# Three narrow matmuls become a wide and a narrow one in the recurrent mixer's input projection, and three steps of attention move

## The chip, the cores and the metric

The kernel runs on one core of one Trainium2 chip. The metric is device time in microseconds (us). The five engines named in the traces are PE (TensorE, matrix products; PEld is its weight load), DVE (VectorE), ACT (ScalarE), POOL (GpSimd) and SP (SyncE, which only issues transfers here). Each takes its instructions in order; semaphores tie the engines together.

## The reference

A trunk of two layers over 256 tokens and 2048 features, in float32. Layer 0 is attention with 16 query heads and 4 key heads of 128 features; layer 1 is a recurrent block; each is followed by a gated feed-forward part. Cut to what the change touches:

```python
h = rms_norm(x, norm_mix[i])
# layer 0
q = apply_axial_rope(rms_norm(q, q_gain), cos, sin) * (HEAD_DIM ** -0.5)   # per head
sc = jnp.einsum('bqkgd,bskd->bkgqs', q_blk, k)
p = jax.nn.softmax(sc, axis=-1);  o = jnp.einsum('bkgqs,bskd->bqkgd', p, v)
# layer 1
xb, yb = jnp.split(h @ w_in, 2, axis=-1)           # (256, 2048) @ (2048, 4096)
yb = jax.nn.gelu(yb, approximate=True)
xb = depthwise_conv_centred(xb, conv_w, conv_b)
out = (rg_lru_forward(xb) + rg_lru_backward(xb)) * yb;  mix = out @ w_out
```

## The kernel before

**Precision.** Every product is made of three: a float32 operand is split into a rounded part hi and a remainder lo, and x·w is taken as xh·wh + xl·wh + xh·wl. Weights come from memory as tiles `raw` of 128x1024 (eight 128x128 blocks; the text calls such a tile a half, since two make the 2048 rows of one projection); ACT makes `hi` (line 135), DVE makes `lo` (line 136). `raw`, `hi` and `lo` each have a ring of five buffers here. Activations lie as `xg`, a tile of 128x512 for each of 16 row blocks k, with the rounded 256 tokens in its left half and the remainders in its right half.

**Two ways to take the three products.** Attention's projections use `blocks` (lines 264 to 274): for a pair of row blocks, hi of the first against all 512 columns (line 272), lo of the first and lo of the second against the left 256 columns (line 270), hi of the second against 512. The left half of the PSUM bank then holds xh·wh, the right half xl·wh + xh·wl, and `evac` (lines 350 to 354) adds the halves: ACT copies the right half to a tile in SBUF, DVE adds the left half to it. The recurrent mixer's projection uses `project_sums` (lines 287 to 296) with `three` (lines 282 to 285): three matmuls of 256 columns for every row block, all summed in the left half of the bank, so that what follows reads the sum from PSUM. The right half is scratch for what follows.

**The recurrent mixer.** 32 column tiles of `w_in` are projected: 16 for the x branch, 16 for the gate branch y. A loop over nine rounds takes two x tiles of the next block and two y tiles of this block in each. `conv_branch` (lines 813 to 826) multiplies the projection by the row `nr.row` (1/rms of the tokens, line 818), and runs the four taps of the convolution with the bank's right half as accumulator (lines 820 to 823); `xs` is the split result. `gelu_branch` (lines 829 to 834) multiplies by the same row. Each block has four gate products (128 output columns by two, `three` again, from `xs` and the gate weights `ghi`, `glo` that POOL splits), and then sigmoids, decays and scans on ACT, DVE and POOL.

**The order.** PE's order is written by the program. A step counter goes up once for each row block in a projection; `later(n, fn)` puts a function on a list, due n steps on, and at each step at most one due entry runs, the earliest entered first. `USUAL` (line 51) holds such distances for the query heads 0 to 13: the sums of squares 17 steps after the head's projection, the scores 22 (heads 0 to 5 have 32 to 24 instead, `EARLY`), the turn of the probabilities 17 after the scores, the product with the values 8 after the turn, and the split of the query. Heads 14 and 15 have `LATE`. The other engines' order is set by a scheduler that works from estimated times.

**A query head** (`attend`, lines 623 to 684): `sums` transposes y on PE (line 639) and squares it on ACT (641); `scores` makes the scores on PE, then on DVE and ACT the head's factor f = 1/rms (648, and `rsqrt`, lines 474 to 483), the row maximum (651) times f (652), the exponentials (657, by way of 493), the reciprocal of their sums (659), the scaled probabilities `pr` (661); `turn` transposes these on PE (667) and splits them as `pT` (669, 670); `values` multiplies them by the values (675).

## Time and profile before

| | us |
|---|---|
| median of 3 runs | 1970.33 (1969.58 to 1970.8) |
| the profiled execution | 1970.78 |
| its span, first to last instruction | 1968.9 |
| query heads, about 57 to 182 us of the span | 125.0, PE busy 121.18 |
| recurrent projections and gates, 961.4 to 1191.3 us | 229.9, PE busy 229.9 |
| DVE busy in the latter | 195.53 |
| ACT busy in the latter | 191.3 |

The span begins at the first instruction on the core, and views give positions in us from there. A row of a group gives line, engine, operation, result<-operands, shapes, count, then busy time, mean duration in ns and the idle time just before. Matmuls overlap on PE: their rows give 283 or 389 ns each, but what a stream costs is the distance from start to start, so this is taken from the timeline. The granted clock is 0.999 over the run.

### The profile page before, as it was taken

Reading aid. Unit: us, or ns where it says so; the run is one execution under the profiler, and the core shown is the slowest. Engines: PE = TensorE matmul, PEld = TensorE weight load, DVE = VectorE, ACT = ScalarE, POOL = GpSimd, SP = SyncE. Lnnn points to the kernel's source line nnn. Section 1 sums busy time; section 2 is a strip of 40 time slices with the busy share of each in tenths; the row PEclk is TensorE's granted clock in tenths of the full one; section 3 lists DMA queues with packets and bytes.
Section 4 is the critical chain, followed back from the end, with each engine's and each line's share of the span. In section 5 each row is a group of like instructions: output and inputs, shape, how many; then the busy total and the mean of one; then the engine's idle time right before and its main releaser. Section 6 shows DMA issues by size and latency. Waiting matters only on the chain.

```text
span 1968.9 us, 28150 instructions
## 1 busy us (share of the span) xinstructions
PE 1957.1 (99%) x9842; PEld 1668.3 (85%) x9842; DVE 1705.4 (87%) x2254; ACT 1388.3 (71%) x2167; POOL 321.7 (16%) x395
## 2 busy tenths in 40 slices
PE   9999999999999999999999999999999999999999
PEld 8888888888888888888999998888888888888887
DVE  7877688899999999998788886897999999999993
ACT  7677586676677766777688887867667676676662
POOL 0443160000000000000456450420000000000000
PEclk9999999999999999999999999999999999999999
DMA  8544655577667776676566555656667776777763
GB/s 308 172 129 129 201 173 193 193 239 221 215 210 227 234 215 219 209 234 216 194 194 192 182 167 175 200 193 214 195 219 217 225 231 209 222 224 225 220 229 117
DMA packets 118079, 402.86 MB, mean 205 GB/s; under 512 B 13232, under 2 KB 13488, under 8 KB 117808
## 3 DMA queue, kind: packets, MB, share of 16 engines
q1 hardware_dynamic: 108432, 384.00, 59.1%
q0 software_dynamic: 9216, 16.78, 4.7%
q8 instruction: 77, 1.26, 0.3%
q14 instruction: 66, 0.54, 0.1%
q10 hardware_dynamic: 288, 0.28, 0.0%
HBM read 382.13 MB, written 2.10 MB: 195 GB/s over the span
## 4 chain that ended last, share of the span: by engine, by line
PE 91%; DVE 4%; POOL 2%; ACT 1%; issue 1%; DMA 1%; ACTq 0%; POOLq 0%; DVEq 0%
PE acc L303 16%; PE acc L304 16%; PE acc L306 16%; PE pm L306 10%; PE pm L304 10%; PE pm L303 10%; PE acc L283 3%; PE acc L284 3%; PE acc L285 3%; DVE lo L136 2%; POOL hb L569 1%; PE pm L284 1%; PE pm L285 1%; PE pm L283 1%; DMA raw<-in_w_qv_dram 0%
## 5 line engine op out<-in xcount | busy, mean ns | idle before, releaser
L136 DVE TENSOR_TENSOR lo<-raw,hi 128x1024 fp32r<-128x1024 f32 (+1 forms) x517 | 631.2, 1251 | 81.0 <-ACT hi L135 80.2
L135 ACT CAST hi<-raw 128x1024 fp32r<-128x1024 f32 (+1 forms) x517 | 527.9, 1046 | 219.3 <-DMA raw<-in_w_down_dram 101.6
L303 PE MATMUL acc<-hi,xg 128*128 128x512 f32 x844 | 328.3, 389 | 0.0
L304 PE MATMUL acc<-hi,xg 128*128 128x512 f32 x844 | 328.3, 389 | 0.0
L306 PE MATMUL acc<-lo,xg 128*128 128x512 f32 x844 | 328.3, 389 | 0.0
L153 ACT CAST hi<-ws 128x1024 fp32r<-128x1024 f32 x188 | 197.9, 1053 | 162.4 <-DVE ws L159 146.0
L156 DVE TENSOR_TENSOR lo<-ws,hi 128x1024 fp32r<-128x1024 f32 x188 | 230.5, 1227 | 35.7 <-ACT hi L153 32.4
L797 POOL DMA_DIRECT2D x<-form x64 | 55.2, 862 | 1069.9 <-ACT form L796 1069.9
L303 PE MATMUL pm<-hi,act 128*128 128x512 f32 x512 | 199.2, 389 | 0.0
L304 PE MATMUL pm<-hi,act 128*128 128x512 f32 x512 | 199.2, 389 | 0.0
L306 PE MATMUL pm<-lo,act 128*128 128x512 f32 x512 | 199.2, 389 | 0.0
L303 PEld LDWEIGHTS acc<-hi,xg 128*128 128x128 f32 x844 | 158.4, 188 | 32.9
L304 PEld LDWEIGHTS acc<-hi,xg 128*128 128x128 f32 x844 | 158.4, 188 | 32.9
L306 PEld LDWEIGHTS acc<-lo,xg 128*128 128x128 f32 x844 | 158.4, 188 | 32.9
L303 PE MATMUL acc<-hi,act 128*128 128x512 f32 x448 | 174.6, 390 | 0.0
L393 ACT COPY two<-one 32x256 f32<-32x256 f32 x420 | 169.6, 404 | 7.0 <-DVE one L385 0.8
L306 PE MATMUL acc<-lo,act 128*128 128x512 f32 x448 | 174.4, 389 | 0.0
L304 PE MATMUL acc<-hi,act 128*128 128x512 f32 x448 | 174.4, 389 | 0.0
L283 PE MATMUL acc<-xg,hi 128*128 128x256 f32 x512 | 144.8, 283 | 0.0
L284 PE MATMUL acc<-xg,hi 128*128 128x256 f32 x512 | 144.6, 282 | 0.0
L285 PE MATMUL acc<-xg,lo 128*128 128x256 f32 x512 | 144.5, 282 | 0.0
L156 DVE TENSOR_TENSOR lo<-raw,hi 128x1024 fp32r<-128x1024 f32 x94 | 114.1, 1214 | 23.0 <-ACT hi L153 23.0
(218 smaller groups left out, 3993.4 us busy)
## 6 DMA issues: line engine op xcount, KB each, us to landing
raw<-in_w_gate_dram SPq DMA_DIRECT2D x176, 512.0 KB, 4.7
raw<-in_w_up_dram SPq DMA_DIRECT2D x176, 512.0 KB, 3.9
raw<-in_w_down_dram SPq DMA_DIRECT2D x176, 512.0 KB, 4.1
raw<-in_w_in_dram SPq DMA_DIRECT2D x64, 512.0 KB, 4.4
raw<-in_w_qv_dram SPq DMA_DIRECT2D x40, 512.0 KB, 3.9
raw<-in_w_o_dram SPq DMA_DIRECT2D x32, 512.0 KB, 3.5
x<-form POOLq DMA_DIRECT2D x64, 256.0 KB, 4.8
raw<-in_w_out_dram SPq DMA_DIRECT2D x32, 512.0 KB, 4.2
```

The costliest lines, as they stand in the source:

```text
L135: behind("cast", act.copy(hi[:, sl], raw[:, sl]))
L136: behind("rest", dve.tensor_tensor(lo[:, sl], raw[:, sl], hi[:, sl].bitcast(F32), ALU.subtract))
L153: behind("cast", act.copy(hi, src))
L156: return lambda: behind("rest", dve.tensor_tensor(lo, src, hi[:].bitcast(F32), ALU.subtract))
L283: pe.matmul(o, hi, x[:, :S], start=start, stop=False)
L284: pe.matmul(o, hi, x[:, S:], start=False, stop=False)
L285: pe.matmul(o, lo, x[:, :S], start=False, stop=stop)
L303: pe.matmul(o, xh, wh, start=start, stop=False)
L304: pe.matmul(o, xl, wh, start=False, stop=False)
L306: pe.matmul(o, xh, wl, start=False, stop=stop)
L393: m = (eng.copy if eng is act else eng.tensor_copy)(to[:, :, :, i, :], of[:, :, :, j, :])
L797: pool.dma_start(out=x_tm[:, a, i[1] * WIDE : (i[1] + 1) * WIDE], in_=t, accum_op=ALU.add)
```

## The change

The input projection of the recurrent mixer goes by `blocks` as attention's does (`project`, and `project_both` for the first two tiles, which go side by side through the halves of the weights): for every pair of row blocks four matmuls, two of 512 columns and two of 256, where there were six of 256. Both halves of the bank now hold a part of the result. So each of the 32 tiles gets an `evac`: a copy of the right half by ACT and an addition by DVE into a new tile `ev` (four buffers), and the multiplication by `nr.row` reads `ev` from SBUF. The right half then serves as scratch as before.

In attention the factor f is made in `sums` and kept until `scores` takes it; and `USUAL` sets the turn 18 steps after the scores (17 before) and the values 9 after the turn (8 before). f's instructions stay the same in number.

```diff
-USUAL = (17, 22, 17, 8, 9)
+USUAL = (17, 22, 18, 9, 9)
...
-    def project_sums(xs, n):
-        banks = [new_acc() for _ in range(n)]
+    def project_both(xs):
+        banks = [new_acc() for _ in range(2)]
         for k0 in range(0, KT, HALF):
             wts = [narrow() for _ in banks]
-            for i in range(0, HALF, HALF // n):
+            for i in range(0, HALF, HALF // 2):
                 for bank, wt in zip(banks, wts):
-                    for k in range(k0 + i, k0 + i + HALF // n):
-                        three(bank[:, :S], *wt[k - k0], xs[k], k == 0, k == KT - 1)
-                        step()
-        return [(bank[:, :S], bank[:, S:]) for bank in banks]
+                    blocks(bank, wt[i : i + HALF // 2], xs, k0 + i)
+        return banks
...
         def sums():
...
+            v = tmp("hv2", (P, 2))
+            dve.scalar_tensor_tensor(v, ms, 1.0 / P, ebt, ALU.mult, ALU.add)
+            factor.append(rsqrt(v, "hf2"))
         def scores():
...
-            v = tmp("hv2", (P, 2))
-            dve.scalar_tensor_tensor(v, ms, 1.0 / P, ebt, ALU.mult, ALU.add)
-            f = rsqrt(v, "hf2")
+            f = factor.pop()
...
     def conv_branch(ct, bank):
-        acc, run = bank
+        t, run = evac(bank, "ev"), bank[:, S:]
...
-        dve.tensor_tensor(b[:, 2 : S + 2], acc, nr.row, ALU.mult)
+        dve.tensor_tensor(b[:, 2 : S + 2], t, nr.row, ALU.mult)
...
     def gelu_branch(ct):
-        acc, y = project_sums(nr.xs, 1)[0]
-        if ct >= KT - 2:
-            y = tmp("gl")
-        dve.tensor_tensor(y, acc, nr.row, ALU.mult)
+        bank = project(nr.xs)
+        y = tmp("gl") if ct >= KT - 2 else bank[:, S:]
+        dve.tensor_tensor(y, evac(bank, "ev"), nr.row, ALU.mult)
         return y
...
-            banks = [] if blk else project_sums(nr.xs, 2)
-            nxt.xcs = [
-                conv_branch(2 * b + 2 + i, banks[i] if banks else project_sums(nr.xs, 1)[0]) for i in range(2)
-            ]
+            banks = [] if blk else project_both(nr.xs)
+            nxt.xcs = [conv_branch(2 * b + 2 + i, banks[i] if banks else project(nr.xs)) for i in range(2)]
```

PE at the start of a y tile in the steady part of the recurrent mixer, before (`acc` is the bank, `xg` the activations of a row block, `hi` and `lo` the weights):

```order
L283 MATMUL acc_10952<-xg_8920,hi_10954 128x256
L284 MATMUL acc_10952<-xg_8920,hi_10954 128x256
L285 MATMUL acc_10952<-xg_8920,lo_10955 128x256
L283 MATMUL acc_10952<-xg_8923,hi_10954 128x256
L284 MATMUL acc_10952<-xg_8923,hi_10954 128x256
L285 MATMUL acc_10952<-xg_8923,lo_10955 128x256
```

The same tile with the change (the next pair of row blocks begins in the fifth row):

```order
L272 MATMUL acc_10744<-xg_8920,hi_10746 128x512
L270 MATMUL acc_10744<-xg_8920,lo_10747 128x256
L270 MATMUL acc_10744<-xg_8923,lo_10747 128x256
L272 MATMUL acc_10744<-xg_8923,hi_10746 128x512
L272 MATMUL acc_10744<-xg_8926,hi_10746 128x512
```

Six rows for a pair of row blocks became four, in the same place among the gates.

DVE behind the end of that y tile, before (`xs` the split convolution, `pm` the gates' banks, `L833` the multiplication of y):

```order
L357 CAST xs_10949<-xc_10944 128x256
L358 TENSOR_TENSOR xs_10949<-xc_10944,xs_10949 128x256
L833 TENSOR_TENSOR acc_10952<-acc_10952,row_9427 128x256
L136 TENSOR_TENSOR lo_11173<-raw_11171,hi_11172 128x1024
L890 SCALAR_TENSOR_TENSOR pm_10817<-sq_11021,pm_10817 128x256
L890 SCALAR_TENSOR_TENSOR pm_10869<-sq_11037,pm_10869 128x256
```

and with the change (`L351` is the addition of evac, `L832` the multiplication):

```order
L355 CAST xs_10741<-xc_10736 128x256
L356 TENSOR_TENSOR xs_10741<-xc_10736,xs_10741 128x256
L136 TENSOR_TENSOR lo_10931<-raw_10929,hi_10930 128x1024
L889 SCALAR_TENSOR_TENSOR pm_10620<-sq_10803,pm_10620 128x256
L889 SCALAR_TENSOR_TENSOR pm_10665<-sq_10815,pm_10665 128x256
L351 TENSOR_TENSOR ev_10822<-acc_10744,ev_10822 128x256
L889 SCALAR_TENSOR_TENSOR pm_10620<-sq_10838,pm_10620 128x256
L889 SCALAR_TENSOR_TENSOR pm_10665<-sq_10850,pm_10665 128x256
L832 TENSOR_TENSOR acc_10744<-ev_10822,row_9401 128x256
```

What DVE does for y moved behind the next split of weights, and is two rows instead of one.

PE at head 0's turn (`pr_896`, rows of line 667), early in the projection of head 4, before:

```order
L272 MATMUL acc_1005<-xg_117,hi_1007 128x512
L270 MATMUL acc_1005<-xg_117,lo_1008 128x256
L667 MATMUL pm_1014<-ident,pr_896 128x128 x4
L270 MATMUL acc_1005<-xg_120,lo_1008 128x256
L272 MATMUL acc_1005<-xg_120,hi_1007 128x512
L639 MATMUL pm_1024<-ident,hy_904 128x128 x2
```

and with the change:

```order
L272 MATMUL acc_1005<-xg_117,hi_1007 128x512
L270 MATMUL acc_1005<-xg_117,lo_1008 128x256
L638 MATMUL pm_1014<-ident,hy_904 128x128 x2
L270 MATMUL acc_1005<-xg_120,lo_1008 128x256
L272 MATMUL acc_1005<-xg_120,hi_1007 128x512
L667 MATMUL pm_1030<-ident,pr_896 128x128 x4
```

The turn stands one row block later, and the transposes for head 2's sums, which stood behind it, now stand ahead of it.

More of the change, by code (lines that the diff above doesn't have):

```diff
@@ L634, in attend @@
         ms = tmp("ms", (P, 2))
+        factor = []
         def sums():
```

## The prediction

> **What bounds the kernel now.** I read the page first, then the windows of the two stretches that the change touches, then the timeline of PE inside them. The page's busy times and the chain that ended last:
>
> ```profile
> span 1968.9 us, 28150 instructions
> PE 1957.1 (99%) x9842; PEld 1668.3 (85%) x9842; DVE 1705.4 (87%) x2254; ACT 1388.3 (71%) x2167; POOL 321.7 (16%) x395
> PE 91%; DVE 4%; POOL 2%; ACT 1%; issue 1%; DMA 1%; ACTq 0%; POOLq 0%; DVEq 0%
> ```
>
> PE is the bound of the whole run; a matmul that becomes cheaper shortens it, unless its feeding fails. The windows, first the recurrent projections, then the query heads, then the stretch behind the projections:
>
> ```profile
> core 0: us, PE busy (x) PEld busy (x) DVE busy (x) ACT busy (x) POOL busy (x), PEclk, DMA share, GB/s
> 961.40:1191.30 229.90, 229.90 (x1925) 229.83 (x1924) 195.53 (x322) 191.30 (x322) 124.94 (x146) 1.00 0.57 181
> 57.00:182.00 125.00, 121.18 (x756) 105.97 (x755) 100.69 (x225) 88.99 (x250) 59.52 (x60) 1.00 0.43 135
> 1192.00:1230.00 38.00, 38.00 (x169) 31.46 (x168) 26.70 (x37) 23.97 (x30) 0.00 (x0) 1.00 0.61 194
> ```
>
> In the first PE has no gap, with DVE at 85% and ACT at 83% beside it. In the second 3.8 us of PE are idle.
>
> **Part 1, the matmuls.** Removed: 32 tiles x 16 row blocks x 3 = 1536 matmuls of 256 columns. Added: 512 of 512 columns and 512 of 256. The gates' 384 of 256 stay. Their price is the distance from start to start. For the narrow ones it is the window's 229.9 us over 1924 matmuls (1920 and four short ones), 0.1195 us, so 0.717 for the six of a pair of row blocks. The order that the change takes over runs in attention's projections; PE's timeline there, in a quiet place (first and last of 17 pairs) and between other work:
>
> ```profile
> 24.60 0.63 PE L272 MATMUL acc<-xg,hi 128*128 128x512 f32 x2
> ...
> 35.74 0.63 PE L272 MATMUL acc<-xg,hi 128*128 128x512 f32 x2
> ...
> 100.69 0.63 PE L272 MATMUL acc<-xg,hi 128*128 128x512 f32 x2
> ...
> 101.38 0.63 PE L272 MATMUL acc<-xg,hi 128*128 128x512 f32 x2
> ...
> 102.09 0.63 PE L272 MATMUL acc<-xg,hi 128*128 128x512 f32 x2
> ```
>
> Each row holds the last matmul of a pair and the first of the next, so rows are one pair apart: (35.74 - 24.60)/16 = 0.696 us, and 0.69 to 0.71 where other matmuls come between. A pair thus gets 0.021 us cheaper. There are 32 x 8 = 256 pairs: 5.4 us at 0.696, 4.4 at 0.70. Gates break in some of the streams, so I take 4.8. The bounds: 0.71 throughout leaves 1.8; the third window, all of 512 columns, has 38.0/168 = 0.226 for one, so that a pair would be 2 x 0.226 + 2 x 0.1195 = 0.691 and the gain 6.7.
>
> The Trainium skill has a lower price for what is saved: TensorE: Matmul & The Clock Gate, Back-to-back issue gap, gives 262 cycles for 256 columns and 518 for 512 at 2.4 GHz, a fixed cost of 6 cycles for each matmul. As an estimate by that page, 512 matmuls fewer would save 512 x 2.5 ns = 1.3 us. The trace's 0.1195 us is 13 ns above 256 columns at that clock, so the rows speak for the larger gain.
>
> **Part 2, the evac and what it hides behind.** Added for each tile: a copy on ACT and an addition on DVE, both of a shape that the queries already have. The rows of these, of the two multiplications that change their source, and of two splits that tell what a source in SBUF does:
>
> ```profile
> L352 ACT COPY hy<-acc 128x256 f32<-128x256 f32 x17 | 6.3, 370 | 5.1 <-PE acc L272 5.0
> L353 DVE TENSOR_TENSOR hy<-acc,hy 128x256 f32<-128x256 f32 x17 | 7.1, 417 | 1.0 <-ACT hy L352 0.8
> ...
> L358 DVE TENSOR_TENSOR xs<-xc,xs 128x256 fp32r<-128x256 f32 x16 | 14.3, 894 | 0.2
> L818 DVE TENSOR_TENSOR cb<-acc,row 128x256 f32<-128x256 f32 x16 | 6.6, 414 | 0.1
> L833 DVE TENSOR_TENSOR acc<-acc,row 128x256 f32<-128x256 f32 x14 | 6.0, 428 | 8.5 <-PE acc L285 8.5
> ...
> L358 DVE TENSOR_TENSOR act<-acc,act 128x256 fp32r<-128x256 f32 x14 | 5.8, 415 | 0.1
> ```
>
> So ACT gets 32 x 0.37 = 11.8 us, DVE 32 x 0.417 = 13.3 us. The multiplications (lines 818 and 833) now read two tiles in SBUF. The split of xs does that too, and takes 0.894 us where the same split from PSUM takes 0.415; a bound for each multiplication is therefore 0.41 to 0.89, and for the 32 of them 0 to 15 us more. POOL works through more than half of this stretch, and I expect about half of that. The Trainium skill says the same of the cause (SBUF — State Buffer, Who interferes with whom): a DVE instruction with two SBUF inputs contends with a POOL instruction that reads SBUF, and the later one waits out the whole of the other. The two rows of line 358 agree.
>
> Is this on the path? One steady block, and what stands around the tightest split of weights in it, from the timelines of DVE and PE:
>
> ```profile
> 1063.70:1092.35 28.65, 28.65 (x242) 28.65 (x241) 24.87 (x41) 24.05 (x41) 15.92 (x19) 1.00 0.59 182
> ...
> 1079.87 1.40 DVE L358 TENSOR_TENSOR xs<-xc,xs 128x256 fp32r<-128x256 f32 x1
> ...
> 1082.74 0.43 DVE L833 TENSOR_TENSOR acc<-acc,row 128x256 f32<-128x256 f32 x1 [1.47 <-PE acc L285]
> 1084.42 1.22 DVE L136 TENSOR_TENSOR lo<-raw,hi 128x1024 fp32r<-128x1024 f32 x1 [1.24 <-ACT hi L135]
> ...
> 1094.78 0.28 PE L283 MATMUL pm<-xs,ghi 128*128 128x256 f32 x1
> ```
>
> A block is 28.65 us and would be 28.65 - 32 x 0.0205 = 28.0. ACT needs 24.05 + 4 x 0.37 = 25.5 of it. DVE needs 24.87 + 4 x 0.417 = 26.5, with the slower multiplications up to 28.5, by my middle value 27.5. The lo that ends at 1085.64 is for the second half of an x tile, whose first matmul stands ten row blocks ahead of the gate product at 1094.78: PE needs it at about 1091.2, so the lead is 5.5 us here, and it is larger for the seven other halves of a block (the ring holds five). DVE's waits of 1.47 and 1.24 us shrink when DVE is late, since both are for PE and ACT. With some 6.5 steady blocks, DVE would have to take 28.0 + 5.5/6.5 = 28.85 us for each before the lead is used up and PE stops. I therefore put the evac at nothing; its cover is this lead, and without it what exceeds 28.0 would be paid block by block. What is late next is the convolution and the end of y, which have room: the split xs that ends at 1081.27 is first needed by the gate product at 1094.78. Behind the projections DVE is busy 26.7 of 38 us, so a debt is worked off there.
>
> **Part 3, attention.** The waits of PE and of its weight loads, from the view of waits, and the two places with the longest stalls in the first and in a later head:
>
> ```profile
> PE pm L667 <- ACT pr L661: 2.7, 4, 1.6
> ...
> PE pm L284 <- DVE pT L670: 1.0, 4, 0.3
> ...
> PEld pm L667 <- ACT pr L661: 5.6, 10, 1.9
> PEld pm L284 <- DVE pT L670: 2.9, 7, 0.6
> ...
> 81.65 0.28 PE L270 MATMUL acc<-xg,lo 128*128 128x256 f32 x1
> 83.51 0.95 PE L667 MATMUL pm<-ident,pr 128*128 128x128 f32 x4 [1.58 <-ACT pr L661]
> ...
> 144.30 0.28 PE L270 MATMUL acc<-xg,lo 128*128 128x256 f32 x1
> 145.06 0.94 PE L667 MATMUL pm<-ident,pr 128*128 128x128 f32 x4 [0.48 <-ACT pr L661]
> ```
>
> Ten turns and seven products with the values hold the weight load, 8.5 us in all. PE's own idle time in front of them is 3.7 us, but a matmul that starts late also loses the overlap with the one before it: from 144.30 to 145.06 pass 0.76 us where 0.12 would do, a loss of 0.64 against 0.48 shown. So the price of these waits lies between 3.7 and 8.5, nearer to the latter. One step is half a pair, 0.35 us. Head 0's turn also gets the transposes of line 639 ahead of it (four a row block before, now two of another head): 0.35 + 0.2 = 0.55 of its 1.9. The nine other turns share 3.7 us, 0.41 each, of which a step takes up to 0.35: 1.9 for those where the wait is that long. The seven products share 2.9 and get one more step behind their turn: 2.0 of it. That is 4.4 us. f's instructions keep their number; on the path they could come earlier by at most what is left of the waits, or push others back by about as much as one step gains, so the bounds for attention are 0 and 8.5. I take 4.0, because the scheduler also reorders a few rows of DVE and ACT here and some of that will be late.
>
> **The sum.** 4.8 + 4.0 = 8.8 us off the profiled execution's 1970.78, whose span leaves 1.9 us outside that nothing here touches: 1962.0. That execution was 0.45 above the median of 1970.33, so the median should be 1961.6.
>
> **The rivals.**
>
> *DVE becomes the bound of the recurrent stretch* (the slower one). Multiplications at 0.89 us and evac's additions make 28.5 us a block; if DVE also keeps its waits for PE and ACT, 1.47 + 1.24, it takes 31.2. PE then stops for 6.5 x (31.2 - 28.0) - 5.5 = 15.3 us: 1961.6 + 15.3 = 1977. It decides from 28.85 us a block, and turns the sum around from 30.2. For it: 894 ns in the row of xs. Against it: a DVE that runs late doesn't wait for what is early. 6%; a mild form, 29.5 us and 4 us lost, 1965.8: 9%.
>
> *Attention gives nothing*, because the chain from scores to pr moves with PE and the wait goes from the turn to the values: 1970.33 - 4.8 = 1965.5. For it: f and the maximum stay in one queue behind splits of 1.2 us. Against it: the waits are short, near to one step. 12%.
>
> *The wide stream isn't cheaper*: pairs at 0.71, as in the row at 102.09, because of gates and more waits on semaphores: 1970.33 - 1.8 - 4.0 = 1964.5. 13%. By the page named above this part would give 1.3 us and the time be 1965.0.
>
> **How the numbers follow.** The forecast has 60%. 1961.6 is its time; its own range is 1958 to 1965. Downwards the bounds give 1970.33 - 6.7 - 6.5 = 1957; upwards the range takes in all rivals but the first: 1968. Within 0.2% (3.9 us, about what a measurement of this kernel can tell from no change) lies 1966.4 to 1974.3. Each of the milder rivals alone stays just below that, so faster has the forecast and most of theirs, 82%; two of them together end within it, 12%; slower is the first rival, 6%.
>
> **What would show it.** Right: the recurrent stretch has some 225 us with PE without gaps and pairs 0.697 apart; DVE busy about 210 there; the lead at the tightest split still above 2 us; PEld's waits for pr and pT at about half of 8.5. Wrong: PE rows with "<-DVE lo" or "<-ACT hi" between 980 and 1230; multiplications by the row at 0.8 us or more; waits for pr that stay at 5.6.

## The result, and the profile after

The changed kernel takes 1967.1 us in the median (14 runs, 1965.9 to 1967.8) against 1970.6 of the kernel before (14 runs, 1969.5 to 1972.0): a ratio of 0.998 with a 95% interval of 0.9972 to 0.9988. So 3.5 us were gained where the prediction had 8.7. The profiled execution took 1967.46 us; its page begins:

```profile
span 1965.4 us, 27183 instructions
PE 1952.5 (99%) x9330; PEld 1641.2 (84%) x9330; DVE 1713.6 (87%) x2286; ACT 1395.1 (71%) x2199; POOL 317.5 (16%) x395
```

PE is busy 4.6 us less than before, and still 99% of the span. For what follows the span is cut in two. The first cut is the first product of the key heads' squares with ones, the second the last product with the values, the end the last matmul. PE's timeline at these three places, before:

```profile
48.28 0.59 PE L585 MATMUL pm<-hsq,ones 128*128 128x256 f32 x2
...
203.31 0.28 PE L285 MATMUL pm<-pT,kv 128*128 128x256 f32 x1
...
1964.41 0.39 PE L306 MATMUL acc<-lo,act 128*128 128x512 f32 x1
```

and after:

```profile
48.72 0.59 PE L583 MATMUL pm<-hsq,ones 128*128 128x256 f32 x2
...
202.39 0.28 PE L285 MATMUL pm<-pT,kv 128*128 128x256 f32 x1
...
1960.93 0.39 PE L304 MATMUL acc<-lo,act 128*128 128x512 f32 x1
```

The stretch **A**, from the first cut to the second, holds the query heads: 203.31 - 48.28 = 155.03 us before, 153.67 after. The stretch **R**, from there to the end (start 1964.41 plus 0.39), holds all the rest: 1761.49 before, 1758.93 after. So attention gave 1.36 us and the recurrence, the only part of R that the change touches, 2.56; together 3.9. What lies ahead of the first cut is the same code in all kernels of this study and takes 47.0 to 48.7 us from one execution to the next. That is more than most of the experiments change. The granted clock goes with it: the six executions with 47.0 to 47.2 us have a clock of 1.00 there, and ten of the twelve with 48.1 to 48.7 us show 0.50 for 3.4 us between 7 and 12 us (in the other two the matmul rows are as long, 628 ns for 397, but the clock's record begins behind them). A and R carry no such scatter: over the six kernels here that have the change's attention at 18 and 9, A is 153.67 to 153.81. They are compared below beside the medians.

**Recurrence.** The window of the recurrent stretch, after:

```profile
960.70:1187.80 227.10, 225.41 (x1413) 202.12 (x1412) 205.54 (x352) 196.22 (x348) 117.97 (x145) 1.00 0.56 181
```

It is 227.1 us long where it was 229.9, and PE, without a gap before, now has 1.7 us of gaps in it. They are in one place. PE's timeline where the first gate product comes, after:

```profile
983.24 0.39 PE L272 MATMUL acc<-xg,hi 128*128 128x512 f32 x1
984.58 0.47 PE L272 MATMUL acc<-xg,hi 128*128 128x512 f32 x1 [0.95 <-DVE xc L823]
...
986.39 0.28 PE L283 MATMUL pm<-xs,ghi 128*128 128x256 f32 x1
987.41 0.39 PE L284 MATMUL pm<-xs,ghi 128*128 128x256 f32 x1 [0.74 <-DVE xs L356]
```

From 983.24 to 984.58 pass 1.34 us where 0.23 would do: a tile waits for its bank, which the convolution of an earlier tile still uses. From 986.39 to 987.41 pass 1.02 us where 0.12 would do: the first gate product, whose first matmul needs the rounded part of `xs` alone, waits at its second one for the remainder of the first tile's convolution (line 356). About 2.0 us are lost in both. The rest of the recurrence runs as forecast: the pairs of row blocks are 0.697 us apart in the median, and a steady block takes 28.06 us where it took 28.67. One such block after, and the groups of the two multiplications:

```profile
1064.94:1093.00 28.06, 28.06 (x178) 25.23 (x177) 25.96 (x45) 24.61 (x45) 14.07 (x18) 1.00 0.58 185
...
L818 DVE TENSOR_TENSOR cb<-ev,row 128x256 f32<-128x256 f32 x16 | 13.7, 859 | 0.0
L832 DVE TENSOR_TENSOR acc<-ev,row 128x256 f32<-128x256 f32 x14 | 5.9, 418 | 0.0
```

PE has no gap; DVE is busy 26.0 of 28.06 us in this block. The multiplication of the convolution doubled in price, that of y did not.

**Attention.** The view of waits between 24 and 205 us, after:

```profile
PEld pm L284 <- DVE pT L670: 4.1, 9, 0.8
PEld pm L667 <- ACT pr L661: 2.9, 4, 1.3
```

The waits of the weight loads for pr fell from 5.6 to 2.9 us, those for pT rose from 2.9 to 4.1: 1.5 us less in all, and A is 1.36 shorter.

### The profile page after: what moved, and what is told of

Same layout as the page of the kernel before. It is cut to its first block, busy times and chain, and to the rows that moved or that the text cites. A ratio compares the mean times of both kernels' runs of the same rounds, so it can differ in the third digit from the quotient of the medians.

```text
span 1965.4 us, 27183 instructions
## 1 busy us (share of the span) xinstructions
PE 1952.5 (99%) x9330; PEld 1641.2 (84%) x9330; DVE 1713.6 (87%) x2286; ACT 1395.1 (71%) x2199; POOL 317.5 (16%) x395
## 4 chain that ended last, share of the span: by engine, by line
PE 91%; DVE 4%; POOL 2%; issue 1%; ACT 1%; DMA 1%; SPq 0%; ACTq 0%; POOLq 0%; DVEq 0%
PE acc L304 16%; PE acc L301 16%; PE acc L302 16%; PE pm L302 10%; PE pm L304 10%; PE pm L301 10%; PE acc L272 6%; PE acc L270 3%; DVE lo L136 1%; POOL hb L567 1%; PE pm L284 1%; PE pm L285 1%; PE pm L283 1%; POOL hq L568 0%; POOL hq L569 0%
## 5 line engine op out<-in xcount | busy, mean ns | idle before, releaser
L272 PE MATMUL acc<-xg,hi 128*128 128x512 f32 x896 | 293.7, 399 | 2.9 <-DVE xg L411 1.9
L270 PEld LDWEIGHTS acc<-xg,lo 128*128 128x128 f32 x896 | 169.1, 189 | 36.7 <-DVE lo L136 1.2
L270 PE MATMUL acc<-xg,lo 128*128 128x256 f32 x896 | 186.0, 282 | 0.4 <-DVE lo L136 0.4
L272 PEld LDWEIGHTS acc<-xg,hi 128*128 128x128 f32 x896 | 141.8, 190 | 3.5 <-DVE xg L411 2.1
```

The costliest lines, as they stand in the source:

```text
L270: pe.matmul(acc[:, S:], w, xs[k][:, :S], start=False, stop=stop)
L272: pe.matmul(acc, w, xs[k], start=(k == 0), stop=stop)
```

## The experiments

Each run is told with its median, its ratio to the kernel before on the same chip, and the stretches A and R of its profiled execution. That kernel has medians of 1970.6 to 1971.05 us on these chips, so the medians of two runs can differ by some 0.4 us for that alone.

### The two parts alone: e_att and e_proj

The kernel before with the attention's edits only, the factor f made in `sums` as in the change:

```diff
-USUAL = (17, 22, 17, 8, 9)
+USUAL = (17, 22, 18, 9, 9)
```

> The kernel before with the attention's two edits alone (the factor of the queries made with the sums; turn and values one step later); the recurrent projection as before. Theory, read from the two traces (recurrent projections begin at 960.73 us instead of 961.66): this part is worth 0.9 us, so 1969.7 us, because the waits for pr were exchanged for waits for pT at the values. Rival, the prediction's own sum: 4.0 us, so 1966.6. A second rival, that the shorter time in the recurrence comes from these edits too (another placement of the later work), would put it below 1966.

And the change with the attention as it was, f made in `scores` again:

```diff
-USUAL = (17, 22, 18, 9, 9)
+USUAL = (17, 22, 17, 8, 9)
```

> The changed kernel with the attention as before (factor made with the scores, turn and values at the old steps); the recurrent projection in 512- and 256-column matmuls. Theory, from the traces (recurrent stretch 229.67 to 227.03 us): 2.6 us faster than before, so 1968.0. Rival, the prediction's sum for the matmuls: 4.8 us, so 1965.8. If the two parts add up, the gains of this run and of the run with the attention's edits alone sum to the 3.5 us of the whole change; if they depend on each other, they do not.

| | median | ratio (95%) | A | R |
|---|---|---|---|---|
| before | 1970.6 | | 155.03 | 1761.49 |
| the change | 1967.1 | 0.998 (0.9972 to 0.9988) | 153.67 | 1758.93 |
| e_att | 1970.4 | 0.9996 (0.9987 to 1.0005) | 153.76 | 1761.48 |
| e_proj | 1968.5 | 0.9985 (0.9976 to 0.9994) | 155.00 | 1758.88 |

Each part moves its own stretch and leaves the other as it was, so the parts add up: 1.3 us from attention, 2.6 from the projection. The medians agree, though for e_att the interval takes in no change. My reading of 0.9 us for attention was too low by the 0.44 us by which the two executions differed at the first cut.

### What the opening of the recurrence waits for: e_open and e_gl

The first two tiles go side by side, so their two copies, additions and multiplications fall due together; that was my first suspect. e_open keeps these two tiles as before the change, with the old `project_sums`:

```diff
-            banks = [] if blk else project_both(nr.xs)
+            banks = [] if blk else project_sums(nr.xs, 2)
...
-        t, run = evac(bank, "ev"), bank[:, S:]
+        t, run = bank[:, :S] if ct < 2 else evac(bank, "ev"), bank[:, S:]
```

> The changed kernel, but with the first two tiles of the recurrence (the two made side by side) as before: three 256-column matmuls for each product into one half of the bank, no copy and no addition afterwards, the first multiplication reading the bank. All other tiles as in the change. Theory: the two stalls of TensorE at 983.2 and 986.4 us (1.1 and 1.0 us) come from the two copies, two additions and slower multiplications that all fall due at once where the two tiles end together; without them 2.1 us come back, less 2 tiles x 8 pairs x 0.020 us = 0.3 us for the dearer matmuls: 1.8 us faster than the change, 1965.3. Rival: the stalls come from the late w_in transfer, which ScalarE's cast waits for (4.36 us against 2.56 before), with or without the copies: then they stay, and the time is 1967.1 to 1967.5.

1966.0 us, ratio 0.9975 (0.9966 to 0.9984), A 153.72, R 1758.92: the same R as the change, so this theory fell. The profiled execution took 1967.0 us; that the median lies 1.1 us under the change's is not explained by either stretch. The part ahead of the first cut could do it, but only one execution of each kernel has a trace. The timelines of e_open, ACT's cast of the half that is waited for and the first gate product:

```profile
977.87 1.05 ACT L135 CAST hi<-raw 128x1024 fp32r<-128x1024 f32 x1 [3.41 <-DMA raw<-in_w_in_dram]
...
987.04 0.38 PE L284 MATMUL pm<-xs,ghi 128*128 128x256 f32 x1 [1.49 <-DVE xs L358]
```

The stall for the bank is gone and the one at the gate has grown in its place, from 0.9 to 1.65 us. In the changed kernel the same cast waits too. Two windows of 5 us, what SP issues, and ACT and DVE behind it:

```profile
960.00:965.00 5.00, 5.00 (x29) 4.32 (x29) 4.58 (x11) 3.37 (x10) 1.61 (x4) 1.00 0.03 11
...
975.00:980.00 5.00, 5.00 (x31) 4.33 (x30) 3.42 (x3) 1.80 (x3) 5.00 (x5) 1.00 0.99 358
...
968.63 1.94 SPq L845 DMA_DIRECT2D graw<-in_w_gates_dram  x4
970.68 5.95 SPq L130 DMA_DIRECT2D raw<-in_w_in_dram  x5
...
978.20 1.06 ACT L135 CAST hi<-raw 128x1024 fp32r<-128x1024 f32 x1 [4.36 <-DMA raw<-in_w_in_dram]
979.16 1.06 ACT L820 ACTIVATE acc<-cb,pk 128x256 f32<-128x256 f32 x2
...
979.29 1.24 DVE L136 TENSOR_TENSOR lo<-raw,hi 128x1024 fp32r<-128x1024 f32 x1 [1.58 <-ACT hi L135]
980.45 0.87 DVE L823 SCALAR_TENSOR_TENSOR acc<-cb,pk,acc 128x256 f32<-128x256 f32 x2
```

The last two columns of a window are the DMA engines' busy share and GB/s. From 960 to 965 almost nothing moves (0.03); from 968.6 everything is asked for at once, four loads of gate weights ahead of the first half of `w_in`, and the engines are full (0.99). The half arrives for the cast at 978.20, 7.5 us after its issue. DVE takes its instructions in order, and the convolution's taps (line 823) stand behind the split of that half.

Before the change that half was late too. ACT, DVE and PE there:

```profile
974.64 1.06 ACT L820 ACTIVATE acc<-cb,pk 128x256 f32<-128x256 f32 x2
978.26 1.05 ACT L135 CAST hi<-raw 128x1024 fp32r<-128x1024 f32 x1 [2.56 <-DMA raw<-in_w_in_dram]
...
985.17 0.41 DVE L358 TENSOR_TENSOR xs<-xc,xs 128x256 fp32r<-128x256 f32 x1
...
987.05 0.28 PE L284 MATMUL pm<-xs,ghi 128*128 128x256 f32 x1
```

ACT made the first tap of both tiles (line 820) ahead of the late half, and the remainder of the first tile was ready before PE asked for it. With the change these taps stand behind the late half. Counted from the second cut, this remainder is ready at 782.3 us before and at 785.0 after, 2.7 us later; without its stall for the bank PE would ask for it 0.7 us earlier than before. The greater part is thus the chain that came later, and not PE that came earlier. But the taps are not the one cause: in e_open they are ahead of the late half again, and the remainder, now with a split of weights ahead of it in DVE's queue, is ready at 784.9. Nor is the arrival: in e_proj the cast comes 0.6 us earlier than in the change, and its stalls are the same (1.1 and 0.9 us).

e_gl puts two of the gate loads behind the first half of `w_in`:

```diff
-        sync.dma_start(out=raw, in_=w["w_gates"][b, :, 4 * g : 4 * g + 4, :])
+        d = sync.dma_start(out=raw, in_=w["w_gates"][b, :, 4 * g : 4 * g + 4, :])
+        if n in (2, 3):
+            follow(d, newest["load"])
...
-            load_gates(4 * b + g + GATE_BUFS)
+            later(8 if b == 0 and g < 2 else 0, partial(load_gates, 4 * b + g + GATE_BUFS))
...
-                    load_gates(g)
+                    later(41 if g > 1 else 0, partial(load_gates, g))
```

> The changed kernel with two of the first four loads of gate weights (of 256 KB each, gates 2 and 3 of the first block) put behind the next load of w_in in SP's queue instead of ahead of it; the next two gate loads follow later too. The run with the old opening left a stall of 1.65 us at gate 0, so the copies and additions were not its cause. New theory: the opening is set by transfers. They are idle from about 960 to 968.6 us, then run full (0.99 of 16 engines, 358 GB/s from 975 to 980), and ScalarE's cast waits until 978.2 for half a tile of w_in that was issued behind 1 MB of gate weights; VectorE's in-order queue has the convolution of the first tiles behind that half. 0.5 MB less ahead of it is 1.5 us at 351 GB/s: the cast comes at 976.7, the two stalls (1.1 and 1.0 us) shrink by up to 1.5 us together or each, and the kernel is 1 to 2 us faster than the change. Rival: the convolution's own chain on VectorE (about 9 us without a gap) sets it, or gate 2 then waits for its weights: no gain.

1966.7 us, ratio 0.9979 (0.9971 to 0.9988), A 153.75, R 1758.32: 0.6 us less than the change, below the 1 to 2 expected. ACT and PE of e_gl:

```profile
974.97 1.05 ACT L135 CAST hi<-raw 128x1024 fp32r<-128x1024 f32 x1 [1.47 <-PE acc L272]
...
985.35 0.35 PE L283 MATMUL pm<-xs,ghi 128*128 128x256 f32 x1 [0.32 <-DVE xs L355]
986.46 0.38 PE L284 MATMUL pm<-xs,ghi 128*128 128x256 f32 x1 [0.75 <-DVE xs L356]
```

The cast comes 2.8 us earlier, counted from the first cut (974.97 - 48.29 against 978.20 - 48.72), and no longer waits for a transfer. The stall for the bank is gone. The gate still waits, for 1.5 us in all from start to start: DVE works from 974.3 us to the gate with one gap of 0.3 us. So both halves of the expectation hold in part: with the earlier transfer the first stall goes, and the second stands behind DVE's full queue. One row there is long: the cast of `xs` that ends at 985.20 takes 1.51 us beside POOL's split of gate weights, and the next one 0.28 us without it.

### The price of the multiplication, and the room on DVE: e_psum and e_dve

e_psum writes evac's sum back into the bank, so that line 818 reads the bank:

```diff
-    def evac(acc, tag):
+    def evac(acc, tag, o=None):
...
-        dve.tensor_tensor(t, acc[:, :S], t, ALU.add)
-        return t
+        o = t if o is None else o
+        dve.tensor_tensor(o, acc[:, :S], t, ALU.add)
+        return o
...
-        t, run = evac(bank, "ev"), bank[:, S:]
+        t, run = evac(bank, "ev", bank[:, :S]), bank[:, S:]
```

> The changed kernel with the convolution's sum written back into the bank's left half, so that the multiplication by the row reads the bank instead of SBUF, as before the change; one more row in the bank instead of SBUF, nothing else. It measures the disputed price of the multiplication: 859 ns mean in the change against 414 before. If two inputs in SBUF are what made it dear, the mean is back at about 415 ns, VectorE is 16 x 0.44 = 7.1 us less busy in the recurrence, and as the steady blocks are set by TensorE (28.06 us each) the time changes by no more than the opening: 0 to 1 us. If the extra time is only a queue ahead of it that the profile counts in, the mean stays above 0.7 us.

1966.4 us, ratio 0.9976 (0.9966 to 0.9986), A 153.78, R 1758.29: 0.6 us less than the change, all of it in the opening (0.4) and the last block (0.2); the steady blocks stay at 28.06 us. The multiplication is back at 412 ns in the mean. One of them after the change, with POOL's split of gate weights beside it, and the same two in e_psum:

```profile
1041.37 2.27 POOL L847 TENSOR_TENSOR glo<-graw,ghi 128x512 fp32r<-128x512 f32 x1
1042.42 1.51 DVE L818 TENSOR_TENSOR cb<-ev,row 128x256 f32<-128x256 f32 x1
```

```profile
1039.87 2.28 POOL L848 TENSOR_TENSOR glo<-graw,ghi 128x512 fp32r<-128x512 f32 x1
1040.91 0.41 DVE L819 TENSOR_TENSOR cb<-acc,row 128x256 f32<-128x256 f32 x1
```

With both inputs in SBUF the multiplication ends only after POOL's instruction (1043.93 after 1043.64); with one in the bank it passes beside it in 0.41 us. The Trainium skill has this rule (SBUF — State Buffer, Who interferes with whom: whoever comes second waits out the other's whole instruction), and the two pairs of rows agree. Of the 16 rows of line 818 in the change six take 1.51 us, each beside such a split, and nine 0.41 to 0.49. Line 832 has two inputs in SBUF as well and kept 418 ns: in the steady blocks it falls where POOL works on no split.

e_dve loads DVE further, with two more multiplications for each y tile, whose results are overwritten:

```diff
-        dve.tensor_tensor(y, evac(bank, "ev"), nr.row, ALU.mult)
+        t = evac(bank, "ev")
+        for _ in range(2):
+            dve.tensor_tensor(bank[:, S:], bank[:, :S], t, ALU.mult)
+        dve.tensor_tensor(y, t, nr.row, ALU.mult)
```

> The changed kernel with two more VectorE multiplications (128x256, one input from the bank) for each tile of the recurrence's second half, into the free half of the bank, whose results are overwritten: 4 x 0.42 = 1.7 us more of VectorE for each block of 28.06 us, and later banks. It measures the cover on which the prediction put its price of nothing. If a lead of 4 to 5 us at the splits covers VectorE's added work, as the prediction has it, the block stays at 28.1 us and the time within 1 us of the change. If VectorE is already what bounds a block (25.3 of 28.06 us busy, and waits in order besides), the block grows by up to 1.7 us, 12 us over 7 blocks.

1975.4 us, ratio 1.0023 (1.0014 to 1.0032), A 153.81, R 1767.18: 8.3 us more than the change. An early steady block, still at 28.06 us, and PE's waits from 1000 us on:

```profile
1036.60:1064.66 28.06, 28.06 (x179) 25.24 (x177) 27.30 (x49) 24.00 (x44) 14.61 (x18) 1.00 0.56 178
...
PE pm L283 <- DVE h L900: 4.5, 1, 4.5
...
PE acc L272 <- DVE act L356: 1.6, 3, 0.7
```

From gate to gate three steady blocks take 28.06 us each, the next two 28.54 and 28.92, and 4.6 us are lost at the third gate product of the last block. Behind that stall the granted clock is 0.50 for 3.4 us. Without the four stalls, 6.7 us in all, 1.6 of the 8.3 us are left; as an estimate, this is what the lower clock costs.

So an overload is covered for some blocks, as the prediction said. But the lead of the weight splits, which it counted on, is not what ran out: PE waits for `act` (line 356) and `h` (line 900), no row of PE waits for a split, and each split of the steady blocks still ends at least 2.4 us ahead of its first matmul. The four added rows of a block are 1.7 us by their durations; DVE's busy time in the same blocks rose by 0.7 to 1.3 us (27.30 against 26.62, 27.29 against 25.96). They also hold y's bank longer, so the run does not show that DVE's time alone stops PE. It does show that the change stands within four such rows a block of a limit.

### Which step of attention gives what: e_f, e_step, e_val2

e_f undoes the two distances and keeps the early factor:

```diff
-USUAL = (17, 22, 18, 9, 9)
+USUAL = (17, 22, 17, 8, 9)
```

> The changed kernel with turn and values back at the old steps, the factor still made with the sums. Theory: the earlier factor does nothing, since the scheduler leaves its rows where they were: from the first key's sums to the last value the stretch is that of the kernel before (155.0 us against 153.7 in the change), 1.3 us slower than the change, so 1968.4. Rival: the factor carries the gain of the part (then 1967.1), and the steps nothing.

e_step keeps the distances and makes the factor with the scores, as before:

```diff
-            f = factor.pop()
+            v = tmp("hv2", (P, 2))
+            dve.scalar_tensor_tensor(v, ms, 1.0 / P, ebt, ALU.mult, ALU.add)
+            f = rsqrt(v, "hf2")
```

> The changed kernel with the factor made with the scores as before, turn and values one step later as in the change. Theory: the steps carry the whole 1.3 us of the attention's part, so this is the change's time within 0.2 us in the stretch from the first key's sums to the last value (153.7 us). Rival: without the earlier factor, the probabilities are later and the waits for pr return: 155 us there, 1.3 us slower.

e_val2 has the values two steps later than the change:

```diff
-USUAL = (17, 22, 18, 9, 9)
+USUAL = (17, 22, 18, 11, 9)
```

> The changed kernel with the attention's values two steps (0.70 us) later still, the turn where the change has it. Theory: the values wait for the split of the turned probabilities (pT), 0.1 to 0.8 us in ten heads, 3.9 us in all; two more steps cover all but about 0.1 us of it: 3.8 us faster than the change, 1963.3. Rival: the scheduler moves that split later with the values that need it, or a bank of PSUM that is held longer makes the next product wait: no gain, 1967.1 or more.

| | median | ratio (95%) | A | R |
|---|---|---|---|---|
| e_f | 1968.4 | 0.9986 (0.9976 to 0.9996) | 156.00 | 1758.93 |
| e_step | 1967.2 | 0.9978 (0.9969 to 0.9987) | 153.80 | 1758.95 |
| e_val2 | 1964.8 | 0.9968 (0.9956 to 0.9981) | 151.70 | 1758.92 |

The early factor gives nothing with the new distances (153.67 with it, 153.80 without). With the old ones A is 1.0 us longer with it (156.00 against 155.00 in e_proj), but no wait grew: those of the weight loads for pr are 5.6 us in both, those for pT 2.4 against 2.8. A window inside the stretch, first e_f, then e_proj (the column before the last two is the granted clock):

```profile
85.00:86.00 1.00, 1.00 (x5) 0.90 (x4) 1.00 (x1) 1.00 (x6) 0.94 (x2) 0.50 0.72 270
...
85.00:86.00 1.00, 1.00 (x7) 0.82 (x7) 1.00 (x2) 1.00 (x7) 0.97 (x1) 1.00 0.67 262
```

From 84 to 87 us the clock is 0.50 in e_f, and with the same order of matmuls it falls 1.4 us behind e_proj there. So its longer A does not show a cost of the early factor; the medians, 1968.4 and 1968.5, show none either. The distances carry the attention's part. Two more steps for the values give 2.0 us, not the 3.8 expected: the weight loads' waits for pT fell by 3.2 us (4.1 to 0.9), but those for pr rose by 1.1 (2.9 to 4.0).

### Turn alone, values alone: e_t18v8 and e_t17v9

Both have the factor with the scores. e_t18v8 moves only the turn:

```diff
-USUAL = (17, 22, 18, 9, 9)
+USUAL = (17, 22, 18, 8, 9)
```

> The changed kernel with the factor made with the scores as before, the turn one step later, the values at the old 8 steps behind it. Compared with the run that has 18 and 9 (153.8 us from the first key's sums to the last value). Theory: the later turn puts pT's split behind the next weight split in VectorE's queue (the order of the rows shows it for nearly every head), so with 8 steps the values wait longer: up to 0.35 us more in each of some ten heads, 155.5 to 157 us, no better than the kernel before (155.0); the time 1.7 to 3 us above the change. Rival: the turn carries the gain, and the stretch is 153 to 154.5 us.

e_t17v9 moves only the values:

```diff
-USUAL = (17, 22, 18, 9, 9)
+USUAL = (17, 22, 17, 9, 9)
```

> The changed kernel with the factor made with the scores and the turn at its old step (17), the values one step later (9). Here pT's split stays ahead of the weight split in VectorE's queue for nearly every head, as before. Theory: the waits for pr stay as before (about 5 us in all on TensorE), those for pT fall by up to 0.35 us a head: 153.3 to 154.3 us from the first key's sums to the last value, so the values' step by itself gives about what both moves give together. Rival: without the turn's step nothing is gained, 155.0 us.

| A, us (factor with the scores) | values 8 behind the turn | values 9 behind it |
|---|---|---|
| turn 17 | 155.00 (e_proj) | 151.00 (e_t17v9) |
| turn 18 | 153.71 (e_t18v8) | 153.80 (e_step) |

The medians are 1966.6 (ratio 0.998, 0.9971 to 0.9989) for e_t18v8 and 1964.2 (0.9969, 0.9957 to 0.9981) for e_t17v9. Both expectations were off: the turn alone gives 1.3 us, no loss; the values alone give 4.0 us, not 1. And the two don't add: with the values moved, the turn's step takes 2.8 us back. The weight loads' waits, first e_t18v8, then e_t17v9:

```profile
PEld pm L284 <- DVE pT L668: 5.6, 7, 1.4
...
PEld pm L665 <- ACT pr L659: 1.6, 2, 1.3
```

```profile
PEld pm L665 <- ACT pr L659: 2.7, 4, 1.9
...
PEld pm L284 <- DVE pT L668: 1.2, 2, 0.9
```

The turn's step changes pr's waits into pT's (5.6 us for pT); without it both are small. One head in the middle shows how. ACT, DVE and PE from its turn on, in the changed kernel:

```profile
144.22 0.60 PE L667 MATMUL pm<-ident,pr 128*128 128x128 f32 x4
144.72 1.03 ACT L135 CAST hi<-raw 128x1024 fp32r<-128x1024 f32 x1
145.77 0.57 ACT L669 CAST pT<-pm 128x512 fp32r<-128x512 f32 x1
...
146.90 1.22 DVE L136 TENSOR_TENSOR lo<-raw,hi 128x1024 fp32r<-128x1024 f32 x1
...
148.11 0.68 DVE L670 TENSOR_TENSOR pT<-pm,pT 128x512 fp32r<-128x512 f32 x1
...
148.85 0.39 PE L284 MATMUL pm<-pT,kv 128*128 128x256 f32 x1 [0.18 <-DVE pT L670]
```

and the same head in e_t17v9:

```profile
143.09 0.60 PE L665 MATMUL pm<-ident,pr 128*128 128x128 f32 x4
143.73 0.59 ACT L667 CAST pT<-pm 128x512 fp32r<-128x512 f32 x1 [0.43 <-PE pm L665]
...
145.04 0.69 DVE L668 TENSOR_TENSOR pT<-pm,pT 128x512 fp32r<-128x512 f32 x1
145.65 1.22 DVE L136 TENSOR_TENSOR lo<-raw,hi 128x1024 fp32r<-128x1024 f32 x1
...
146.66 0.28 PE L283 MATMUL pm<-pT,kv 128*128 128x256 f32 x1
```

In the change the copy of pT stands behind a cast of weights on ACT, and its split behind a split of weights on DVE; both are 1.0 to 1.2 us long. From the turn to the end of the split pass 4.6 us. In e_t17v9 pT goes ahead of both, and it takes 2.6 us. Over heads 4 to 12 the median of this time is 3.3 us before, 3.8 in e_t18v8, 4.5 in the change and 2.8 in e_t17v9. The scheduler ranks these rows anew for every set of distances: one step of PE's order moved a row of 0.7 us behind one of 1.2 us in another engine's queue. That the waits for pr fall too when only the values move (from 5.6 to 2.7 us) I did not foresee, and its cause isn't settled.

### What beats both kernels: e_b1, e_b2, e_b3, e_b4, e_b5

e_b1 takes e_val2 (18 and 11) and lets the first block's gates come later; e_b2 has the turn at 19, the values at 11 and the loads of e_gl besides:

```diff
-WHEN_FIRST = (37, 40, 44, 48, 51, 54, 58, 61, 63, 65, 67, 69, 71, 75, 79)
+WHEN_FIRST = (41, 44, 47, 50, 52, 54, 58, 61, 63, 65, 67, 69, 71, 75, 79)
```

> The changed kernel with the values two steps later (as in the run with the values later), and the first block's four gates 4, 4, 3 and 2 steps later (steps 41, 44, 47, 50 instead of 37, 40, 44, 48). The loads of gate weights stay where the change has them. Theory: the stall of 1.0 us at the first gate only means that the gate comes before VectorE's queue has reached the convolution's split; 4 steps (1.4 us) of projection put ahead of it cover it. From the first key's sums to the end: 1910.6 (values later) less 1.0, so 1909.6; the time 3.0 us under the change, 1964.1. The stall of 1.1 us for a bank stays, since its cause is the same chain and not the gates. Rival: the gates that come later lengthen the block's end, or the stall only moves to the next instruction that needs the chain: 1910.6.

> The changed kernel with all that the runs so far point to: turn one step and values two steps later still (19 and 11), the first block's gates at steps 41, 44, 47, 50, and two of the first gate loads behind the next w_in load. Theory: attention under 151.7 us from the first key's sums to the last value, since four waits of 0.29 us for the second half of the probabilities go too (150.5 to 151.7); in the opening both stalls go (2.1 us). From the first key's sums to the end 1908.0 to 1908.6 against 1912.6 of the change: 4.0 to 4.6 us under it, 1962.6 to 1963.1. Rival: the later turn brings the waits for pT back (attention 152 to 153), and the gates' later loads make gate 2 wait: 1910 or more.

e_b3 is e_b2 with the sum written into the bank, as in e_psum. e_b4 is e_b3 with the attention of e_t17v9 (17 and 9, factor with the scores), and e_b5 has its values one step later still (17 and 10). Their diffs are those above.

> The version with the later turn and values, later first gates and reordered gate loads, and besides the convolution's sum written back into the bank so that the multiplication reads the bank. Theory: the steady blocks are set by TensorE at 28.06 us and the opening's stalls are down to 0.3 us, so 7 us less of VectorE's time is worth 0 to 0.3 us: 1908.5 to 1908.9 us from the first key's sums to the end, 1962.0 to 1962.4. Rival: VectorE still sets part of the opening and of the last block, and it gains 0.5 us or more.

> All that gained in the runs so far, and nothing else: the projection of the change; factor made with the scores; turn at its old step, values one step later (17, 9); first gates at steps 41, 44, 47, 50; two of the first gate loads behind the next w_in load; the convolution's sum written into the bank. If the parts are independent stages, they add: 151.0 us in the attention instead of 151.3 in the last combined run, 1907.5 us from the first key's sums to the end, 1962.0. Rival: the attention's gain changes the start of the recurrence (transfers, queues): 1908.5 or more.

> The same with the values two steps later than before and the turn unmoved (17, 10). With (17, 9) the values start 3.6 us after the turn and the split of pT ends 2.8 us after it, so the room is already there in most heads: no more than 0.5 us further gain from the two heads that still wait (0.75 and 0.13 us). If the later values push pT's split or their own copies behind other work in the queues, it is 1 to 3 us slower than with (17, 9).

| | median | ratio (95%) | A | R |
|---|---|---|---|---|
| e_b1 | 1963.9 | 0.9962 (0.9949 to 0.9976) | 151.77 | 1758.49 |
| e_b2 | 1962.4 | 0.9956 (0.9943 to 0.9968) | 151.62 | 1757.20 |
| e_b3 | 1962.3 | 0.9958 (0.9946 to 0.9971) | 151.31 | 1756.53 |
| e_b4 | 1962.1 | 0.9954 (0.9941 to 0.9968) | 151.02 | 1756.71 |
| e_b5 | 1962.8 | 0.9960 (0.9948 to 0.9973) | 152.28 | 1757.01 |

e_b1 took the gate's stall away, but the stall for the bank grew from 1.1 to 1.9 us: 0.4 us gained, the rival's outcome for the most part. Both stalls go only when the transfers are reordered too: e_b2 gains 1.7 us in R, of about 2.0 that were lost, and with the cheaper multiplication e_b3 gains 2.4. e_b4 is the fastest in the median, 8.7 us under the kernel before and 5 under the change; e_b2, e_b3 and e_b4 lie within each other's intervals. The window of e_b4 over the recurrence:

```profile
960.70:1187.80 227.10, 227.10 (x1419) 203.84 (x1418) 203.99 (x349) 199.84 (x353) 118.41 (x145) 1.00 0.57 184
```

PE has no gap there any more. One step more for the values (e_b5) makes A 1.3 us longer again. That is the size of the second expected outcome, but not its way: the weight loads' waits for pT fell once more (1.2 to 0.5 us), and those for pr rose from 2.7 to 5.1.

## Why the prediction was right or wrong

**Part 1, the matmuls: right.** Pairs are 0.697 us apart, and a steady block fell by 0.61 us. With the 2.0 us lost at the opening, the recurrence's 2.56 us make 4.6, against 4.8 forecast. 512 matmuls fewer saved 9 ns each. The estimate of 1.3 us worked out from the Trainium skill (TensorE: Matmul & The Clock Gate, Back-to-back issue gap) does not agree with this; the measurement decides. The section gives its formula for an isolated matmul, and these run in a stream. The rival of a stream that isn't cheaper is out with it.

**Part 2, the evac: right in the steady blocks, wrong at their opening.** The multiplication of the convolution costs 859 ns, at the upper bound of 0.41 to 0.89, that of y the lower. DVE takes 26.0 to 27.0 us in the steady blocks measured, where 27.5 was my middle value; the splits of weights still come at least 4.0 us ahead of PE there, and no wait for `lo` or `hi` stands in the recurrent stretch. So the cost of nothing held there, but e_dve shows that its reason was not the right one: with more work for DVE, PE stops for `act` and `h` while the splits still lead by 2.4 us. A step that failed is "What is late next is the convolution and the end of y, which have room". That was read from a steady block. At the opening there is hardly any room: before, the remainder of the second tile ended at 987.05 us and was needed at 987.40. With the change the chain to the first tile's remainder ended 2.7 us later and PE came 0.7 us earlier: of 4.6 us saved 2.0 were turned into two waits. e_open shows that taking evac's work away there does not bring the remainder forward, e_gl and e_b2 that the order of the transfers has a part in the stalls, and e_psum that the dearer multiplication has one of 0.4 us. Which row of DVE's queue makes up the rest, no run isolates.

**Part 3, attention: the larger step that failed.** The prediction gave the turns 2.4 us (0.55 + 1.9). pr's waits of the weight loads did fall, by 2.7 us. It gave the products with the values 2.0 us, because they "share 2.9 and get one more step behind their turn". Their waits rose by 1.2 instead. A distance in PE's order was counted as room, while the chain that has to fit into it was taken as fixed; but the scheduler put pT's copy and split behind a cast and a split of weights when the turn moved, and the chain grew from 3.3 to 4.5 us. The values' step alone gives the 4.0 us of the sum (e_t17v9), and the turn's step takes 2.8 of them back; that the two numbers meet is luck, since the forecast's sum has both moves in it. The rival that attention gives nothing came true by about two thirds in its size. Of its mechanism one half holds, "the wait goes from the turn to the values"; the other, that the chain to pr moves with PE, does not, since the waits for pr did fall.

**The early factor** was given no price of its own, rightly with the new distances; with the old ones its price stays open, since e_f's trace has a stretch at half the clock in A.

**The sum.** 4.6 - 2.0 + 1.4 = 4.0 us, against 3.9 in A and R together and 3.5 in the medians. The forecast and its own range of 1958 to 1965 failed; the wide range of 1957 to 1968 holds the time. One mild rival came true by two thirds, and the loss at the opening was not among the rivals. Of the signs that were set, the pairs and the lead came out right; the waits for pr and pT stayed at 7.0 us where half of 8.5 was expected, PE has gaps at the opening, and the multiplication above 0.8 us, a sign of being wrong, came true without a cost in the steady blocks.

## What to carry to other kernels

When one engine's order is fixed and a scheduler ranks the others', a distance in steps is only room if the chain that must fit into it keeps its place in the other queues: look up what stands ahead of it before and after, row by row, for each move alone. A saving that holds in the steady part can be lost where a stretch begins, because the order of the queues and the transfers are others there: follow the first block separately, from the first transfer on. And measure an edit between two landmarks inside the trace, where the start of the program scatters by more than the edit is worth; and compare the granted clock over the same stretch before a difference of 1 us is put down to the edit.

## What the runs showed that I had not expected

- A multiplication of two SBUF tiles on DVE took 1.51 us beside POOL's split of 2.27 us, and 0.41 us when one input lay in the bank, with the same POOL instruction beside it.
- The two distances in attention interact: each alone gains 1.3 and 4.0 us, both together 1.2.
- DVE at 97% of a block (27.30 of 28.06 us) held for three blocks, then cost 0.5 and 0.9 us in the next two and 4.6 us in the last: the price of this overload came late, in waits for `act` and `h` and not for splits of weights.
- The first 47.0 to 48.7 us vary by 1.7 us between executions, with a stretch of 3.4 us at a granted clock of 0.50 in ten of the twelve longer ones. Where A and R have no such stretch, they repeat within about 0.1 us in the traces of kernels that share their code.
- Two traces have such a stretch later: e_f in A, where it looked like a price of the edit, and e_dve behind its stall of 4.6 us.
